# Neighbourhood attention with its projections four half-steps ahead, and modulation weights loaded two blocks at a time

## The chip, the cores and the metric

The kernel runs on one core of one Trainium2 chip. The metric is the device time of one execution in microseconds (us). An execution has five engines that work side by side, each through its own list of instructions in order: TensorE (PE; its weight loads are shown apart as PEld), VectorE (DVE), ScalarE (ACT), GpSimd (POOL) and SyncE (SP), which here only issues DMAs. Instructions wait for each other through semaphores.

## The reference, cut to what matters

The model has two layers over 512 latent tokens and 256 context tokens of width 1024. Layer 0 mixes tokens by neighbourhood attention with 16 heads of 64, layer 1 by a bidirectional recurrence (RWKV-7); each is followed by a mixture of 16 experts. Each layer is modulated: a vector of 6 x 1024 numbers per token kind is computed from a condition.

```
sh1, sc1, gt1, sh2, sc2, gt2 = split(silu(c) @ ada_w[i] + ada_b[i], 6)      # ada_w[i]: 1024 x 6144
h   = rms_norm(x, norm1_g[i]) * (1 + sc1) + sh1
q, k, v = h @ w_qkv;   q, k = rms_norm per head
s_lat = q . k(8 x 16 neighbourhood) * scale + bias(relative row, relative column);   s_ctx = q . k(context) * scale
o   = softmax([s_lat, s_ctx]) @ [v_lat, v_ctx];     x = x + gt1 * (o @ w_o)
x   = x + gt2 * experts(rms_norm(x) modulated by sh2, sc2)
```

The same is done for the context tokens, with c_ctx in place of c and attention to context alone. `ada_w` of the two layers is 50 MB in float32.

## The kernel before, in words

Layer 0's attention is `phase_na`. The 16 heads are taken as 8 pairs `p`. All matmuls of projections and scores are done in split form (a high part and a low part, three matmuls for one product, `passes`).

*Opening.* The input rows are normalised and transposed. `ada(S, 0, 0)` and `ada(S, 0, 1)` (shift and scale of layer 0) run here, with seven buffers of 512 KB for their weights, and then the modulated input is written as `hTh` and `hTl`. `na_consts` (line 217) makes the masks and loads the position biases of all 16 heads into one tile `BT` by 16 DMAs on SP.

*One modulation part.* `ada(S, l, j)` (line 117) computes one of the six parts of layer `l`. Its 1024 x 1024 weights come in 8 blocks of 128 rows, each one DMA of 512 KB on SP. For each block four matmuls (a quarter of the columns each, in a quarter of the rows of the result) go to a PSUM tile, and VectorE adds the result to `acc` (line 137); with the first block a bias is added by four more matmuls (line 133) and the result copied (line 135). After each block the generator yields. At the end two transposes and a copy give `modT`. Parts 2 to 5 of layer 0 and all six of layer 1 are left for the attention: 10 parts, 80 steps.

*One projection.* `na_project(S, p)` (line 279) loads and splits the weights (`split_weights`: ScalarE line 252, VectorE line 253), then makes queries and keys of pair `p` in six products of 24 matmuls, yielding after each. After every second product the rows are normalised (ScalarE squares into `sq`, VectorE sums, ScalarE takes the root, VectorE scales, line 305), transposed on TensorE and written as `qT`, `kT` and `kl`. For even `p` six more products give the values of two pairs.

*One pair of attention.* `na_attend(S, p)` (line 345) takes 16 half-steps. Half-steps 0 to 11 make scores (TensorE lines 357 to 367), softmax (VectorE lines 375 to 386, with the bias from `BT` at line 377; ScalarE line 384); transposes follow one step later and values (line 406) two steps later, so half-steps 12 to 15 hold only transposes and values of the last two blocks.

*The order.* `weave` (line 487) advances several generators at given rates in one loop. First projection 0 alone. Then for `p` = 0 to 6: the 16 half-steps of attention `p`, the projection of pair `p + 1` (13 steps if it has values, else 7, spread over the 16), and one modulation step per half-step, until the 80 are used up. Then the projections' memory is given back (`ew.close()`), the gate rows are made, the output weights are loaded and split (`out_weights`, 8 DMAs of 512 KB on SP), and pair 7 is attended alone. Then the rows of x are loaded again, and `out_project` and the experts follow. The order in the program is a priority: a planner puts each engine's instructions in order by it and by when their tiles are free and their inputs expected; on the chip each engine keeps that order. All the loads named here stand in one queue, SP's. A load into a tile of a pool waits until the tile's last users are done.

Of the kernel before, what the change touches and what calls it, by code (L numbers as in the profile page):

```python
# [20 lines left out]
F32 = mybir.dt.float32  # L21
# [10 lines left out]
P = 128  # L32
D = 1024
KD = 8
# [6 lines left out]
H = 16  # L41
# [9 lines left out]
def vap(ap, dims, offset=0):  # L51
    return bass.AP(tensor=ap.tensor, offset=ap.offset + offset, ap=dims)
# [64 lines left out]
def ada(S, l, j):  # L117

    nc, I = S.nc, S.I
    acc = S.small.tile([P, 256], F32, name="adam")  # L120
    adab = S.small.tile([24, 256], F32, name="adab")
    nc.gpsimd.dma_start(adab, I["ada_b"][l].rearrange("(c n) -> c n", n=256))
    for k in range(KD):
        w = S.adaw.tile([P, D], F32, name="adaw")
        nc.sync.dma_start(w, I["ada_w"][l, k * P:(k + 1) * P, j * D:(j + 1) * D])
        ps = S.ps_mm.tile([P, 512], F32, name="mm")[:, :256]
        for q in range(4):
            nc.tensor.matmul(ps[32 * q:32 * q + 32], S.sT[:, k, :], w[:, q * 256:(q + 1) * 256],
                             start=True, stop=(k > 0))
        if k == 0:  # L130
# [86 lines left out]
def na_consts(S, pool):  # L217
    nc, rp = S.nc, S.rp
    S.BT = pool.tile([P, H, 265], F32, name="BT")
    for c in range(16):  # L220
        nc.sync.dma_start(S.BT[8 * c:8 * c + 8], vap(rp, [[31, 8], [465, H], [1, 265]], c))
    S.mL = pool.tile([P, P], BF16, name="mL")
# [58 lines left out]
def na_project(S, p, hT, wp, grp, Q):  # L281
# [11 lines left out]
    Q.k = grp.tile([P, 2, 768], F32R, name="kT")  # L293
    Q.kl = S.kl[p % 2]
    w = split_weights(S, wp, "w", [(i * P, W[:, i * D + p * P:i * D + (p + 1) * P]) for i in range(2)], 3)
    for t in range(0, NT, 2):
        for ps in product(w, t):
            yield
        sq = S.small.tile([P, 2, 256], F32, name="sq", bufs=1)
        nc.scalar.activation(sq, ps, AF.Square)  # L300
# [36 lines left out]

STEPS = 16
STRIP = (0, 64, 192, 256)
# [5 lines left out]
def na_attend(S, p, Q, V, VS, OT):  # L345
# [14 lines left out]
    def scores(u):  # L360
# [5 lines left out]
        if w == 0:  # L366
# [4 lines left out]
            dots(ps[:, 256:512], s, qc, slice(512, 768), True)  # L371
            b = S.BT[:, 2 * p + s, BOFF[j]:BOFF[j] + 1]
            b = bass.AP(tensor=b.tensor, offset=b.offset, ap=[list(b.ap[0]), [-1, 32], [-31, 8]])
# [136 lines left out]
def phase_na(S):  # L510
    nc, tc, I = S.nc, S.tc, S.I
    with ExitStack() as es:
# [6 lines left out]
        S.wraw = ew.enter_context(tc.tile_pool(name="nawr", bufs=2))  # L519
        S.adaw = ew.enter_context(tc.tile_pool(name="naada", bufs=2))  # L520
        S.ps_sc = ea.enter_context(tc.tile_pool(name="ps_sc", bufs=2, space=PSUM))
# [14 lines left out]
        raw = tmp.tile([P, KD, 768], F32, name="raw")  # L536
        adaw, S.adaw = S.adaw, et.enter_context(tc.tile_pool(name="nada0", bufs=7, side="right"))
        rms_rows(S, XN, XN, raw.rearrange("p k t -> p (k t)"))
# [26 lines left out]
        def modulation():  # L565
            for l, js in ((0, range(2, 6)), (1, range(6))):
                for j in js:
                    yield from ada(S, l, j)
        mods = modulation()
        weave(1, (na_project(S, 0, (hTh, hTl), wp, grp, Q[0]), 0, 1))  # L570
        for p in range(7):
            def some():
                for _ in range(STEPS):
                    next(mods, None)
                    yield
            weave(1, (na_attend(S, p, Q[p], Q[p - p % 2].V, Q[p - p % 2].VS, OT), 0, 1),
                  (na_project(S, p + 1, (hTh, hTl), wp, grp, Q[p + 1]), 0, (13 if p % 2 else 7) / STEPS),
                  (some(), 0, 1))
        for _ in mods:
            pass  # L580
        ew.close()
# [4 lines left out]
        ws = out_weights(S, es, I["na_w_o"][0])  # L586
        weave(1, (na_attend(S, 7, Q[7], Q[6].V, Q[6].VS, OT), 0, 1))
        ea.close()
# [1357 lines left out]
```

## Time and profile before

| | us |
|---|---|
| three runs | 2753.96, 2755.37, 2766.93 (median 2755.37) |
| the profiled execution | 2758.18 |
| its span, first to last instruction | 2756.4 |
| TensorE busy, of the span | 2470.2 (90%) |
| VectorE busy | 1327.1 (48%) |
| ScalarE busy | 1004.0 (36%) |
| GpSimd busy | 591.5 (21%) |
| DMA of the hardware queues, as a share of 16 engines | 63.5% |

The profile is that of one execution. "Busy" is the time in which at least one instruction of the engine is under way; matmuls are pipelined, and one that starts 0.12 us after another is shown with a length of 0.28 us, so a busy TensorE need not be at its peak. The granted clock (PEclk) is the share of full speed that TensorE was given: 1.00 is 2.4 GHz and 0.50 is 1.2 GHz. The attention of layer 0 lies from 58 to 534 us of the span.

### The profile page before, as it was taken

The page shows a single profiled execution, that of the slowest core. Times are in us where ns is not written, and L with a number is a line of the kernel's source. Part 1 is how long each engine was busy: PE and PEld are TensorE (multiplying, and loading weights), DVE is VectorE, ACT ScalarE, POOL GpSimd, SP SyncE. Part 2 cuts the span into 40 slices and gives each one's busy share as a digit, 9 for nine tenths or more (in the row PEclk, how much of TensorE's full clock was granted, in tenths as well). Part 3 has the DMA queues.
Part 4 walks back from the last instruction along what each step waited for, and adds up shares of the span by engine and source line. Part 5 has one row for each costly group of instructions (what it writes and reads, how often), then busy time and mean ns, then how long its engine had stood idle before and what let it go on. Part 6 is the DMA issues. An engine that isn't in the chain of part 4 may idle for free. (4 is left out here: it accounts for less than half of the span.)

```text
span 2756.4 us, 44025 instructions
## 1 busy us (share of the span) xinstructions
PE 2470.2 (90%) x16800; PEld 1574.1 (57%) x16800; DVE 1327.1 (48%) x3006; ACT 1004.0 (36%) x2127; POOL 591.5 (21%) x857
## 2 busy tenths in 40 slices
PE   6998999898999999997698697999999977998887
PEld 4876879793333333333388686777777862332222
DVE  6665566642222222225978845666666771221222
ACT  3555556642111101113266634766665431000100
POOL 2100000121000000001656525665655110000000
PEclk9999999998999999998899898999999978999999
DMA  8646440328787878784157866565554369999998
GB/s 246 147 150 187 132 152 15 109 100 327 298 320 312 334 305 329 293 357 172 69 186 241 269 167 130 124 134 125 126 122 125 87 243 378 420 420 421 420 420 342
DMA packets 378371, 637.64 MB, mean 231 GB/s; under 512 B 133832, under 2 KB 301056, under 8 KB 329008
## 3 DMA queue, kind: packets, MB, share of 16 engines
q1 hardware_dynamic: 370944, 609.11, 63.5%
q0 software_dynamic: 7216, 25.70, 2.5%
q8 instruction: 134, 2.20, 0.3%
q14 instruction: 77, 0.63, 0.1%
HBM read 565.11 MB, written 53.88 MB: 225 GB/s over the span
## 5 line engine op out<-in xcount | busy, mean ns | idle before, releaser
L790 PE MATMUL P<-wm,xin 128*64 128x512 f32 x2048 | 494.3, 601 | 25.8 <-DMA wm<-in_moe_w_dram 24.7
L790 PEld LDWEIGHTS P<-wm,xin 128*64 128x64 f32 x2048 | 141.0, 137 | 328.3 <-issue 259.4
L823 PE MATMUL mm<-wm,hidT 128*64 128x512 f32 x1024 | 245.9, 601 | 16.8 <-ACT hidT L807 14.9
L801 ACT ACTIVATE hid<-P 128x512 f32<-128x512 f32 x32 | 19.1, 597 | 563.3 <-PE P L790 563.3
L763 POOL DMA_INDIRECT xg<-xnd,ii x20 | 19.7, 985 | 846.5 <-PE tp L77 571.5
L837 DVE SCALAR_TENSOR_TENSOR Y<-mm,gates,gt 64x512 f32<-64x512 f32 x64 | 48.0, 750 | 283.1 <-PE mm L823 282.4
L260 PE MATMUL mm<-wh,hTh 128*128 128x256 f32 x576 | 173.5, 302 | 1.9 <-ACT hTh L554 1.9
L802 DVE TENSOR_TENSOR hid<-P,hid 128x512 f32<-128x512 f32 x32 | 22.1, 692 | 308.3 <-PE P L790 293.6
L262 PE MATMUL mm<-wh,hTl 128*128 128x256 f32 x576 | 168.4, 293 | 1.9 <-DVE hTl L557 1.9
L261 PE MATMUL mm<-wl,hTh 128*128 128x256 f32 x576 | 168.7, 293 | 0.0
L823 PEld LDWEIGHTS mm<-wm,hidT 128*64 128x64 f32 x1024 | 72.7, 137 | 151.9 <-issue 121.3
L1477 POOL TENSOR_TENSOR Wi<-Wi,Ti 112x30 f32<-112x30 f32 (+14 forms) x240 | 141.4, 589 | 18.8
L1475 POOL TENSOR_TENSOR Ti<-Wi 112x30 f32<-112x30 f32 (+14 forms) x240 | 134.9, 562 | 18.2
L795 PE MATMUL Pc<-wm,xin 128*32 128x512 f32 x1024 | 138.5, 597 | 0.0
L260 PEld LDWEIGHTS mm<-wh,hTh 128*128 128x128 f32 x576 | 114.3, 199 | 11.9 <-issue 8.8
L262 PEld LDWEIGHTS mm<-wh,hTl 128*128 128x128 f32 x576 | 113.6, 198 | 4.5 <-DVE hTl L557 2.8
L1554 PE MATMUL mm<-FR,QF 128*128 128x128 f32 (+1 forms) x768 | 115.1, 294 | 0.4 <-ACT QF L1542 0.4
L261 PEld LDWEIGHTS mm<-wl,hTh 128*128 128x128 f32 x576 | 114.6, 199 | 1.3 <-issue 1.1
L864 DVE TENSOR_TENSOR X<-mm,X 128x512 f32<-128x512 f32 x80 | 52.6, 687 | 111.9 <-PE mm L863 111.7
L1554 PEld LDWEIGHTS mm<-FR,QF 128*128 128x128 f32 x768 | 98.7, 200 | 7.4 <-ACT QF L1542 0.9
L1542 ACT ACTIVATE QF<-mm 64x256 f32<-64x256 f32 x192 | 72.6, 378 | 67.7 <-PE mm L1538 64.3
L1557 DVE TENSOR_TENSOR FT<-mm,eye 64x128 f32<-64x128 f32 x192 | 55.8, 292 | 78.9 <-ACT FT L1556 76.6
(437 smaller groups left out, 5715.6 us busy)
## 6 DMA issues: line engine op xcount, KB each, us to landing
wm<-in_moe_w_dram SPq DMA_DIRECT2D x378, 1024.0 KB
adaw<-in_ada_w_dram SPq DMA_DIRECT2D x96, 512.0 KB
wraw<-in_na_w_qkv_dram SPq DMA_DIRECT2D x32, 256.0 KB
wm<-in_moe_w_dram POOLq DMA_DIRECT2D x6, 1024.0 KB, 10.8
pkd<-sig SPq DMA_DIRECT2D x24, 256.0 KB
pkd<-kka SPq DMA_DIRECT2D x24, 256.0 KB
pkd<-av SPq DMA_DIRECT2D x24, 256.0 KB
sig<-pkd SPq DMA_DIRECT2D x16, 384.0 KB
```

The source lines that it names most:

```text
L260: S.nc.tensor.matmul(ps, xh, wh, start=(k == 0), stop=False)
L261: S.nc.tensor.matmul(ps, xh, wl, start=False, stop=False)
L262: S.nc.tensor.matmul(ps, xl, wh, start=False, stop=(k == n - 1))
L790: nc.tensor.matmul(ps[64 * hf:64 * hf + 64], xin[:, k, cl], w[:, hf * 512:(hf + 1) * 512], start=k == 0, stop=k == KD - 1)
L795: nc.tensor.matmul(Pc[32 * i:32 * i + 32], xinc[:, k, cc], ws[k][i // 2][:, (i % 2) * 512:(i % 2 + 1) * 512], start=k == 0, stop=k == KD - 1)
L823: nc.tensor.matmul(py[64 * hf:64 * hf + 64], hT[:, k % 4, k // 4, :], ws[k][:, hf * 512:(hf + 1) * 512], start=k == 0, stop=k == KD - 1)
L864: nc.vector.tensor_tensor(X[t][:, sl], ps, X[t][:, sl], op=ALU.add)
L1475: nc.gpsimd.tensor_tensor(t, W3[:, i + 1:32, i:i + 1].to_broadcast([112, n, i]), W3[:, i:i + 1, 0:i].to_broadcast([112, n, i]), op=ALU.mult)
L1477: nc.gpsimd.tensor_tensor(W3[:, i + 1:32, 0:i], W3[:, i + 1:32, 0:i], t, op=ALU.add)
L1542: nc.scalar.activation(QF[m][0:64, u], pq[64 * u:64 * u + 64], AF.Copy)
L1554: nc.tensor.matmul(pf[:, h, s0:], QF[m][:, u, h, :], rhs, start=True, stop=True)
L1557: nc.vector.tensor_tensor(F[64:128, :, 64:128], pf[64:128, :, 64:128], S.eye2[64:128, None, :].to_broadcast([64, 2, 64]), op=ALU.add)
```

## The change

It does five things. Attention becomes one generator over all pairs, and the first weave takes only 12 of its half-steps, so that each later weave begins with the last four half-steps of the pair before, and the last stretch has 20 half-steps. `ada` loads two blocks by one DMA of 1 MB and adds up two blocks in PSUM before VectorE reads them: 4 steps per part, 40 in the attention. Four of them go into each of the seven weaves, and the last 12 beside the last stretch at a rate of 0.6 per half-step. The pool of their two tiles moves so that it lives until the last pair is done; the opening has four tiles of 1 MB for seven of 512 KB. The position biases are loaded for each pair, by two DMAs in `na_project`, into a tile with two buffers. `sq` gets a second buffer.

```diff
@@ ada
-    for k in range(KD):
-        w = S.adaw.tile([P, D], F32, name="adaw")
-        nc.sync.dma_start(w, I["ada_w"][l, k * P:(k + 1) * P, j * D:(j + 1) * D])
+    for k in range(0, KD, 2):
+        w = S.adaw.tile([P, 2, D], F32, name="adaw")
+        nc.sync.dma_start(w, I["ada_w"][l, k * P:(k + 2) * P, j * D:(j + 1) * D].rearrange("(i p) n -> p i n", p=P))
         ps = S.ps_mm.tile([P, 512], F32, name="mm")[:, :256]
-        for q in range(4):
-            nc.tensor.matmul(ps[32 * q:32 * q + 32], S.sT[:, k, :], w[:, q * 256:(q + 1) * 256],
-                             start=True, stop=(k > 0))
+        for i in range(2):
+            for q in range(4):
+                nc.tensor.matmul(ps[32 * q:32 * q + 32], S.sT[:, k + i, :], w[:, i, q * 256:(q + 1) * 256],
+                                 start=i == 0, stop=i == 1 and k > 0)
@@ na_consts
-    S.BT = pool.tile([P, H, 265], F32, name="BT")
-    for c in range(16):
-        nc.sync.dma_start(S.BT[8 * c:8 * c + 8], vap(rp, [[31, 8], [465, H], [1, 265]], c))
@@ na_project
+    Q.BT = grp.tile([P, 2, 265], F32, name="BT")
+    for s in range(2):
+        nc.sync.dma_start(Q.BT[:, s], vap(S.rp, [[1, 16], [31, 8], [1, 265]], 465 * (2 * p + s)))
...
-        sq = S.small.tile([P, 2, 256], F32, name="sq", bufs=1)
+        sq = S.small.tile([P, 2, 256], F32, name="sq")
@@ module
-STEPS = 16
+STEPS, LEAD, ADA, LASTADA = 16, 4, 4, 0.6
@@ phase_na
-        S.adaw = ew.enter_context(tc.tile_pool(name="naada", bufs=2))
+        S.adaw = ea.enter_context(tc.tile_pool(name="naada", bufs=2, side="right"))
...
-        adaw, S.adaw = S.adaw, et.enter_context(tc.tile_pool(name="nada0", bufs=7, side="right"))
+        adaw, S.adaw = S.adaw, et.enter_context(tc.tile_pool(name="nada0", bufs=4, side="right"))
...
-        mods = modulation()
+        def attention():
+            for p in range(8):
+                yield from na_attend(S, p, Q[p], Q[p - p % 2].V, Q[p - p % 2].VS, OT)
+
+        def some(gen, n):
+            for _ in range(n):
+                next(gen, None)
+                yield
+        mods, att = modulation(), attention()
         weave(1, (na_project(S, 0, (hTh, hTl), wp, grp, Q[0]), 0, 1))
         for p in range(7):
-            def some():
-                for _ in range(STEPS):
-                    next(mods, None)
-                    yield
-            weave(1, (na_attend(S, p, Q[p], Q[p - p % 2].V, Q[p - p % 2].VS, OT), 0, 1),
-                  (na_project(S, p + 1, (hTh, hTl), wp, grp, Q[p + 1]), 0, (13 if p % 2 else 7) / STEPS),
-                  (some(), 0, 1))
-        for _ in mods:
-            pass
+            n = STEPS if p else STEPS - LEAD
+            weave(1, (some(att, n), 0, 1),
+                  (na_project(S, p + 1, (hTh, hTl), wp, grp, Q[p + 1]), 0, (13 if p % 2 else 7) / n),
+                  (some(mods, ADA), 0, ADA / n))
         ew.close()
...
-        weave(1, (na_attend(S, 7, Q[7], Q[6].V, Q[6].VS, OT), 0, 1))
+        weave(1, (att, 0, 1), (mods, 0, LASTADA))
         ea.close()
```

## Rows read from the trace of the kernel before

**Rows 1.** Busy time of each engine by stretch. Columns: stretch, its length, then for PE, PEld, DVE, ACT and POOL the busy time and the number of instructions, then the granted clock, the busy share of the DMA engines and GB/s.

```profile
58.00:492.00 434.00, 416.01 (x3679) 341.58 (x3680) 261.97 (x754) 238.65 (x463) 35.12 (x78) 0.96 0.45 126
492.00:534.00 42.00, 32.75 (x252) 26.82 (x252) 32.46 (x85) 32.68 (x62) 2.49 (x5) 0.88 0.44 148
534.00:610.00 76.00, 76.00 (x670) 76.00 (x668) 27.27 (x62) 30.72 (x64) 18.94 (x27) 1.00 0.17 66
...
58.00:94.00 36.00, 35.24 (x282) 33.58 (x282) 19.28 (x37) 13.63 (x26) 6.44 (x13) 0.95 0.68 80
...
153.00:267.00 114.00, 110.57 (x1028) 87.33 (x1026) 69.59 (x208) 62.80 (x122) 8.60 (x19) 1.00 0.50 153
283.00:393.00 110.00, 108.31 (x1009) 85.83 (x1013) 67.25 (x200) 61.30 (x120) 7.56 (x17) 1.00 0.52 158
```

**Rows 2.** TensorE's instructions in order of time, from a stretch without a stall. Columns: start, length, engine, line, operation, tiles, form, number merged into the row.

```profile
300.35 0.64 PE L128 MATMUL mm<-adaw,sT 128*32 128x256 f32 x8
300.92 0.28 PE L367 MATMUL sc<-mR,mL 128*128 128x256 bf16 x1
...
305.02 0.28 PE L261 MATMUL mm<-wl,hTh 128*128 128x256 f32 x1
305.14 0.28 PE L262 MATMUL mm<-wh,hTl 128*128 128x256 f32 x1
305.35 0.64 PE L128 MATMUL mm<-adaw,sT 128*32 128x256 f32 x8
```

**Rows 3.** TensorE's instructions in order of time at the end of pair 0; in brackets the idle time before and what ended it.

```profile
137.52 0.28 PE L262 MATMUL mm<-wh,hTl 128*128 128x256 f32 x1
...
142.66 1.09 PE L77 MATMUL tp<-ident,sq 128*128 128x128 f32 x4 [1.88 <-DVE sq L305]
144.78 1.08 PE L128 MATMUL mm<-adaw,sT 128*32 128x256 f32 x8 [1.03 <-DMA adaw<-in_ada_w_dram]
...
148.71 0.58 PE L260 MATMUL mm<-wh,hTh 128*128 128x256 f32 x1
149.09 0.41 PE L261 MATMUL mm<-wl,hTh 128*128 128x256 f32 x1
149.31 0.42 PE L262 MATMUL mm<-wh,hTl 128*128 128x256 f32 x1
```

**Rows 4.** Busy time by stretch, columns as in rows 1, at the ends of pairs 0, 2 and 4.

```profile
140.00:153.00 13.00, 9.26 (x59) 6.07 (x56) 5.66 (x15) 3.98 (x7) 1.30 (x3) 0.61 0.76 241
267.00:283.00 16.00, 11.13 (x78) 7.95 (x81) 7.21 (x21) 5.37 (x10) 1.30 (x3) 0.68 0.62 199
393.00:406.00 13.00, 9.52 (x67) 7.36 (x59) 6.09 (x13) 5.24 (x8) 0.79 (x2) 0.74 0.37 121
```

**Rows 5.** TensorE's waits: engine, line, what it waited for, us in total, times, longest. The first two from 58 to 492 us, then the wait for modulation weights alone in 140 to 152, 262 to 278 and 390 to 400 us.

```profile
PE mm L128 <- DMA adaw<-in_ada_w_dram: 11.2, 9, 2.3
PE tp L77 <- DVE sq L305: 5.6, 3, 1.9
...
PE mm L128 <- DMA adaw<-in_ada_w_dram: 1.9, 2, 1.0
...
PE mm L128 <- DMA adaw<-in_ada_w_dram: 3.0, 2, 2.3
...
PE mm L128 <- DMA adaw<-in_ada_w_dram: 1.6, 1, 1.6
```

**Rows 6.** TensorE's instructions in order of time, in the last pair.

```profile
505.67 0.37 PE L367 MATMUL sc<-mR,mL 128*128 128x256 bf16 x1 [3.66 <-DVE nm L377]
...
509.42 1.12 PE L77 MATMUL tp<-ident,sb 128*128 128x128 f32 x4 [2.10 <-DVE sb L386]
```

**Rows 7.** Groups of instructions from 58 to 492 us: line, engine, operation, tiles, form, number, busy time and mean ns of one, idle time before them.

```profile
L137 DVE TENSOR_TENSOR adam<-mm,adam 128x256 f32<-128x256 f32 x70 | 29.1, 416 | 33.2 <-PE mm L128 32.9
...
L77 PE MATMUL tp<-ident,adam 128*128 128x128 f32 x20 | 4.6, 316 | 0.0
```

**Rows 8.** The loads: first SP's instructions in order of time (start, time to the end of the last merged), then the issues by tile with their number and size.

```profile
43.76 20.79 SPq L221 DMA_DIRECT2D BT<-rpbp  x16
73.99 4.23 SPq L273 DMA_DIRECT2D wraw<-in_na_w_qkv_dram  x4
...
adaw<-in_ada_w_dram SPq DMA_DIRECT2D x96, 512.0 KB
...
wraw<-in_na_w_o_dram SPq DMA_DIRECT2D x8, 512.0 KB
...
BT<-rpbp SPq DMA_DIRECT2D x16, 132.5 KB
```

**Rows 9.** TensorE's instructions in order of time, at the end of the opening's modulation.

```profile
43.07 0.64 PE L128 MATMUL mm<-adaw,sT 128*32 128x256 f32 x8 [0.63 <-DMA adaw<-in_ada_w_dram]
44.41 0.64 PE L128 MATMUL mm<-adaw,sT 128*32 128x256 f32 x8 [0.69 <-DMA adaw<-in_ada_w_dram]
45.58 0.44 PE L77 MATMUL tp<-ident,adam 128*128 128x128 f32 x2 [0.54 <-DVE adam L137]
```

**Rows 10.** Busy time by stretch, columns as in rows 1: the opening's loads, and the loads of x after the last pair.

```profile
10.00:40.00 30.00, 22.40 (x165) 10.17 (x165) 22.86 (x45) 7.66 (x11) 1.51 (x3) 1.00 1.05 381
...
532.00:538.00 6.00, 5.31 (x48) 5.07 (x46) 1.54 (x3) 2.17 (x4) 0.50 (x1) 1.00 0.88 328
```

**Rows 11.** SP's waits from 58 to 492 us, columns as in rows 5.

```profile
SPq L125 <- PE mm L128: 187.7, 68, 14.3
```

More of the change, by code (lines that the diff above doesn't have):

```diff
@@ L217, in na_consts @@
 def na_consts(S, pool):
-    nc, rp = S.nc, S.rp
-    S.BT = pool.tile([P, H, 265], F32, name="BT")
-    for c in range(16):
-        nc.sync.dma_start(S.BT[8 * c:8 * c + 8], vap(rp, [[31, 8], [465, H], [1, 265]], c))
+    nc = S.nc
     S.mL = pool.tile([P, P], BF16, name="mL")
@@ L371, in scores @@
             dots(ps[:, 256:512], s, qc, slice(512, 768), True)
-            b = S.BT[:, 2 * p + s, BOFF[j]:BOFF[j] + 1]
+            b = Q.BT[:, s, BOFF[j]:BOFF[j] + 1]
             b = bass.AP(tensor=b.tensor, offset=b.offset, ap=[list(b.ap[0]), [-1, 32], [-31, 8]])
```

## The prediction, made before the changed kernel was run

> **What bounds the kernel now.** I read the busy times of the page first: TensorE is the fullest engine. Then the busy time by stretch, to find where the changed code lies: the pairs woven with projections run from 58 to 492 us, the last pair alone from 492 to 534, the output projection from 534 to 610 [rows 1]. In the first stretch TensorE is busy 416.0 of 434 us at a mean granted clock of 0.96, and no other engine comes near (VectorE 262, ScalarE 239): this stretch is bound by TensorE's order of work. The DMA engines are at 0.45. In 492 to 534 nothing is full: TensorE 32.8, VectorE 32.5, ScalarE 32.7 of 42 us. From 534 to 610 TensorE is busy all the time. So whatever brings the output projection forward brings all that follows it forward by as much, since everything behind it waits for its tiles.
>
> Busy time of a matmul holds its latency, so I take prices from starts: a projection matmul starts 0.12 us after the one before it, a modulation block (8 instructions) gives way after 0.57 us, and the switch to it costs some 0.09 us (0.21 instead of 0.12 between the two starts) [rows 2].
>
> The lost time in the stretch has one shape. At the end of each even pair (140, 268 and 395 us) the next pair's projection has no value part, so its last q/k product is followed at once by scores that need it. TensorE waits 1.88 us for VectorE's scaled rows, then the next modulation blocks in its order wait for their DMA (1.03 us before the first; 1.9 at this place, 3.0 and 1.6 at the other two [rows 5]), and then matmuls start 0.21 us apart instead of 0.12 [rows 3]: the granted clock has gone to the lower level (1.2 GHz of 2.4) after the idle time. The three places, as length minus busy time times granted clock, lose 13 - 9.26 x 0.61 = 7.4, 16 - 11.13 x 0.68 = 8.4 and 13 - 9.52 x 0.74 = 6.0 us, together 21.8 [rows 4]. The waits of TensorE in the stretch say the same: 11.2 us for modulation weights and 5.6 us for the scaled rows are nearly all of its 18 us [rows 5]. The fourth such place is 501 to 509 us, inside the last pair: 3.66 and 2.10 us idle [rows 6]; that stretch loses 42 - 32.75 x 0.88 = 13.2 us.
>
> **The change part by part.**
>
> *Four half-steps of lead.* The last four half-steps of a pair hold no scores, only transposes and values. With the lead they stand at the head of the next weave, beside the first three half-products of the next projection (3 x 24 x 0.12 = 8.6 us) and one modulation step. From the end of the last product (137.8) to the point where TensorE ran on at 148.7 [rows 3] the old chain took 10.9 us, 1.9 of them waits for DMA; some 9 us of chain now stand over 8.6 + 1.2 us of modulation + about 2 us of tail. That covers it, barely, and the clock stays up with it. I take 85% of 21.8: 18.5 us; bounds 0 and 21.8. Next in line is the next projection's weight split, whose second half waits for a tile that the last product frees.
>
> *Modulation, two blocks at a time.* TensorE has the same instructions, 8 for a block. Before: 80 steps x (0.57 + 0.09) + 10 x 0.99 for bias and transposes (0.57 + 0.09, and 0.33 for the two transposes, 0.32 long and overlapped [rows 7]) = 62.7 us. After: 28 steps beside the projections are 56 x 0.57 + 28 x 0.09 + 7 x 0.99 = 41.4 us, so 21.3 us leave this stretch; 12 steps beside the last pair are 24 x 0.57 + 12 x 0.09 + 3 x 0.99 = 17.7 us. The 40 additions less on VectorE (0.416 us each [rows 7], 16.6 us) are worth nothing while it is busy 262 of 434 us; at most they shorten what the lead covers anyway.
>
> *Slower loads beside the projections.* 4 MB of modulation weights per pair instead of 8: the waits for them outside the three places are 11.2 - (1.9 + 3.0 + 1.6) = 4.7 us [rows 5]; I take 3 of them, bounds 0 and 5.1 (the idle time of 153 to 267 and 283 to 393 [rows 1]).
>
> *Biases per pair.* The 16 issues of 132.5 KB stay 16; before they held the SP queue from 43.8 to 64.6 us, and the weights of pair 1 went out at 74.0 [rows 8]. TensorE lost 0.8 us in 58 to 94, so nothing is gained. Two issues (0.6 us of SP) and 0.27 MB per pair now stand ahead of weights that are needed a weave later, and the pair's own biases have that weave to land in: 0, at most 2 us lost if they push the weights. The second buffer of the squares: 0 to 1 us gained, 0 taken.
>
> *Opening.* Eight loads of 1 MB in four tiles for 16 of 0.5 MB in seven. After the last landing two blocks are to do instead of one (0.64 us at 44.41, then the transposes at 45.58 [rows 9]): +0.6 us, and some more if fewer, larger tiles come free late. I take +1, bounds -1 and +3. The Trainium skill ("DMA: Bandwidth & Descriptors", section "Bandwidth") says to batch DMAs to 1 MiB for three quarters of peak, and its section on the anatomy of one DMA gives about 2 us of fixed cost each; by that, 8 loads fewer would be an estimated 16 us less here. The trace does not agree: half-megabyte loads already run at 381 GB/s with the engines full from 10 to 40 us [rows 10].
>
> *The last pair.* TensorE's useful work there is 32.75 x 0.88 = 28.8 us, and 17.7 come in: 46.5 us against 42. The tail of the pair before replaces the norm chain that it waited for, the 13.2 us of loss fall to some 3.5 (the score chains at the end stay), so 50 us: +8. VectorE gets 12 additions and copies (5 us) on 32.5, so it stays under. The DMA: 12.6 MB of modulation weights and 4.2 MB of output weights [rows 8], some 2.1 MB of it ahead of time; 14.7 MB take 39 us at the 381 GB/s of the opening and 45 at the 328 of 532 to 538 us [rows 10]. Both fit into 50. Bounds 46.5 and 65 (45 us, and 20 for output and modulation loads waiting for each other in SP's one order: an estimate from 12 loads x the 1.6 us that 0.5 MB takes at 328).
>
> **Sum** on the profiled execution (span 2756.4, with 1.8 around it 2758.2): -18.5 - 21.3 - 3 + 1 + 8 = -33.8 us, 2724. The median of the runs is 2755.4, 2.8 lower: I forecast **2721.5**.
>
> **The rivals** (on the median).
> - *Lead without cover.* The planner puts the weight splits or modulation blocks so that the three places still stall: the 18.5 stay, -15.3, **2740**. For it: ScalarE's splits wait for the product's tiles. Against: the work named above is there.
> - *The last pair is paced by its loads*: 62 us instead of 50, -21.8, **2733.5**. For it: SP has one order, and output weights wait there for VectorE's splits.
> - *All cover*: every stall goes and the last pair takes 46.5: -21.8 - 21.3 - 5.1 + 4.5 = -43.7, **2711.5**.
> - *Slower: the last pair's loads run at the pace of the woven pairs.* There 153 GB/s [rows 1], because each load waits for TensorE to give back one of two tiles (187.7 us of SP's waits [rows 11]); TensorE in turn waits for the load, with attention queued behind it and VectorE's splits behind that. 14.7 MB at 153 are 96 us, +54 instead of +8: +12, **2767**. It turns the sign once that stretch passes 84 us (175 GB/s). Against: tiles twice as large hold 2.1 MB ahead.
> - *A shorter opening*: if a load's price is per load and not per byte, eight loads fewer at the 1.34 us between the last blocks [rows 9] take 10.7 us from the opening instead of adding 1, -45.5, **2710**. The full DMA engines of [rows 10] speak against it. (This is the page's rule on batching; its 2 us each would make it 2705.)
>
> **How the numbers follow.** Forecast 0.50 (own range 2714 to 2729); no cover 0.12; last pair paced by loads 0.17; all cover 0.11; slower 0.07; shorter opening 0.03. A measurement can tell about 0.5%, here 13.8 us (below 2741.6 and above 2769.1; part of the 2767 case with worse loads passes it, and I count all of it). Faster: 0.50 + 0.11 + 0.03 and most of the two weak cases (0.05 of 0.12, 0.11 of 0.17) = 0.80; same 0.13; slower 0.07. The range reaches from 2703 to 2746: it leaves out the slower case, the far ends of the two weak ones, and little below.
>
> **What would show it.** Right: no stretch between 90 and 450 us with a granted clock near 0.6, TensorE's wait for modulation weights under 4 us up to the last projection, that projection's end near 450 us instead of 492, the first matmul of the output projection near 500 instead of 534, and the same lengths behind it. Wrong in a step: idle TensorE ahead of the scores of odd pairs (lead); over 60 us between the last projection and the output projection (loads). The whole is wrong if the output projection comes forward but the expert layer's start does not, because a tile is freed later there.

## The result, and the profile after

The changed kernel takes 2722.5 us (median of 4 runs, 2719.1 to 2727.9) against 2758.4 for the kernel before on the same chip: a ratio of 0.987, with an interval of 0.984 to 0.989. The forecast was 2721.5. The profiled execution took 2723.3 (span 2721.5), 34.9 less than that of before, where the sum of the prediction gave 33.8. The sum is right to a microsecond; its terms are not.

The windows of the changed kernel, columns as in [rows 1]: up to the last projection product, then up to the first product of the output projection; then, as places that answer to those of [rows 4], windows around the last scaled rows of pairs 1, 3 and 5, which TensorE now transposes at 137.5, 239.7 and 342.6 us.

```profile
58.00:436.30 378.30, 376.69 (x3419) 328.32 (x3417) 243.61 (x692) 225.43 (x451) 37.37 (x77) 1.00 0.38 113
436.30:499.40 63.10, 53.49 (x526) 36.73 (x524) 40.09 (x112) 35.10 (x70) 3.00 (x6) 0.89 0.74 253
...
137.00:150.00 13.00, 13.00 (x121) 11.32 (x120) 7.23 (x18) 5.59 (x13) 2.09 (x5) 1.00 0.38 122
237.00:253.00 16.00, 16.00 (x143) 13.60 (x142) 8.74 (x22) 5.69 (x13) 2.09 (x5) 1.00 0.42 137
340.00:353.00 13.00, 13.00 (x119) 10.64 (x118) 6.11 (x15) 4.04 (x10) 1.40 (x4) 1.00 0.42 131
```

The three stalls are gone: TensorE is busy all through them, at full clock. In the whole woven stretch, length less busy time times clock was 434.0 - 416.01 x 0.96 = 34.6 us before [rows 1]; it is 378.3 - 376.7 = 1.6 now. But the stretch from the last projection to the output projection has grown from 41.8 to 63.1 us. TensorE's waits say the same: the first line is the only one from 58 to 436 us, where [rows 5] had 11.2 us for weights; the second is the longest from 436 to 499.

```profile
PE mm L260 <- DVE hTl L558: 1.5, 2, 0.8
...
PE mm L129 <- DMA adaw<-in_ada_w_dram: 7.9, 5, 2.6
```

TensorE in that stretch, first a window and the longest of the waits for weights, then the end in order of time:

```profile
452.00:460.00 8.00, 5.60 (x35) 3.71 (x39) 5.14 (x21) 3.17 (x8) 0.00 (x0) 0.59 1.01 361
...
454.25 1.93 PE L129 MATMUL mm<-adaw,sT 128*32 128x256 f32 x16 [2.61 <-DMA adaw<-in_ada_w_dram]
...
482.40 1.07 PE L129 MATMUL mm<-adaw,sT 128*32 128x256 f32 x16 [0.38 <-DMA adaw<-in_ada_w_dram]
483.40 0.63 PE L134 MATMUL mm<-adab,ident 24*32 24x256 f32 x8
483.96 0.65 PE L407 MATMUL po<-PT,V 128*64 128x128 f32 x6
485.26 1.07 PE L129 MATMUL mm<-adaw,sT 128*32 128x256 f32 x16 [0.64 <-DMA adaw<-in_ada_w_dram]
488.68 1.07 PE L129 MATMUL mm<-adaw,sT 128*32 128x256 f32 x16 [2.35 <-DMA adaw<-in_ada_w_dram]
491.69 1.93 PE L129 MATMUL mm<-adaw,sT 128*32 128x256 f32 x16 [1.94 <-DMA adaw<-in_ada_w_dram]
493.56 3.78 PE L154 MATMUL mm<-ident,modT 128*128 128x128 f32 x16
...
499.36 0.36 PE L258 MATMUL mm<-o0h,oh 128*128 128x256 f32 x1
```

One wait, 2.61 us, comes early, and the clock goes to the lower level behind it (0.59 from 452 to 460 us). The last values of attention (line 407) stand at 483.96. Three modulation steps follow, each waiting for its weights. The last of them and the first gate rows (line 154) run at the lower clock: 1.93 us for sixteen matmuls that take 1.07 above.

Behind the attention the lengths are not what they were. From its first to its last product of the hidden layer (`P`) the expert layer 0 takes 610.4 us for 621.9; the recurrence with the routing (from the last scatter of the expert layer 0 to the first product of layer 1) takes 1011.8 for 1001.5. Attention -34.5, experts -11.5, recurrence +10.3: the last two cancel.

### The profile page after: what moved, and what is told of

Same layout as the page of the kernel before. It is cut to its first block, busy times and chain, and to the rows that moved or that the text cites. A ratio compares the mean times of both kernels' runs of the same rounds, so it can differ in the third digit from the quotient of the medians.

```text
span 2721.5 us, 43825 instructions
## 1 busy us (share of the span) xinstructions
PE 2454.3 (90%) x16800; PEld 1582.0 (58%) x16800; DVE 1313.6 (48%) x2958; ACT 993.0 (36%) x2121; POOL 595.7 (22%) x857
## 5 line engine op out<-in xcount | busy, mean ns | idle before, releaser
L258 PE MATMUL mm<-wh,hTh 128*128 128x256 f32 x576 | 168.0, 292 | 2.1 <-ACT hTh L555 2.1
## 6 DMA issues: line engine op xcount, KB each, us to landing
wm<-in_moe_w_dram POOLq DMA_DIRECT2D x6, 1024.0 KB, 10.7
```

Source lines behind the costliest of these rows:

```text
L258: S.nc.tensor.matmul(ps, xh, wh, start=(k == 0), stop=False)
```

## The experiments

All twelve runs beside the two kernels. The first two columns are the starts of the last projection product and of the first output projection product; then the length of the expert layer 0, all from the profiled execution; then the median of the runs.

| kernel | last projection | output projection | expert 0 | median us |
|---|---|---|---|---|
| before | 492.1 | 533.9 | 621.9 | 2756 to 2759 |
| after | 436.3 | 499.4 | 610.4 | 2722.5 |
| e4: before + lead | 466.5 | 512.5 | 623.3 | 2744.6 |
| e7: before + biases per pair | 487.2 | 529.2 | 623.6 | 2756.7 |
| e9: e7 + four single tiles | 466.9 | 510.3 | 623.4 | 2737.8 |
| e6: e7 + two blocks | 460.7 | 501.9 | 611.2 | 2709.8 |
| e11: e6 + lead | 454.2 | 500.1 | 612.1 | 2718.1 |
| e2: after - lead | 452.0 | 510.1 | 610.5 | 2724.9 |
| e1: after, 6 steps per weave | 447.6 | 487.0 | 622.5 | 2721.0 |
| e12: e1 - lead | 461.7 | 502.8 | 623.4 | 2731.5 |
| e10: e1, one `sq` | 448.5 | 491.7 | 611.0 | 2714.2 |
| e5: after, 5 steps, rate 0.25 | 447.4 | 493.4 | 622.7 | 2720.5 |
| e8: after, rate 1.0 | 436.7 | 504.6 | 622.9 | 2735.1 |
| e3: after, later loads left out | 436.9 | 490.8 | 623.5 | 2721.7 (one run) |

### What removed the stalls

**Without the lead** (e2).

```diff
-STEPS, LEAD, ADA, LASTADA = 16, 4, 4, 0.6
+STEPS, LEAD, ADA, LASTADA = 16, 0, 4, 0.75
```

> The changed kernel with LEAD = 0 (and the last 12 modulation steps at 0.75 per half-step, so that they end with the 16 half-steps that are left). Theory (the lead covers the norm chain): TensorE waits again for the scaled rows at the ends of pairs 0, 2, 4 and 6, with the low clock behind it, 4 to 6 us each: time 2738-2746. Rival (the stalls went because the modulation loads are slower and no longer wait there): no stall, time 2722 +- 4.

**The lead alone**, on the kernel before with its single blocks (e4): `attention()`, `some(att, n)` and `n` as in the change, `some(mods, n)` at a rate of one.

> The kernel before with the lead alone (one attention generator, first weave 12 half-steps); modulation in single blocks, 16 per weave, biases all at once. Theory (the lead covers the chain): the three stalls and the one at 501 us go, 22 to 30 us: time 2727-2737. Rival (the modulation loads make the stalls): TensorE waits for modulation weights at the same places, time 2750 or more.

The woven stretch of e2, then of e4, columns as in [rows 1]:

```profile
58.00:452.00 394.00, 390.68 (x3454) 332.79 (x3453) 244.36 (x702) 226.58 (x456) 35.64 (x77) 1.00 0.35 108
```

```profile
58.00:466.50 408.50, 399.51 (x3642) 330.06 (x3643) 256.97 (x744) 235.03 (x455) 36.46 (x78) 1.00 0.47 133
```

Both are at full clock: of the 34.6 us that the stretch lost before, 3.3 are left in e2 and 9.0 in e4. (e4's output projection comes 21.4 us earlier, and its profiled execution is 22.3 us shorter; the median of its ten runs, 2744.6, is only 11 us below that of before and lies between its two forecasts.) That fits a stall with two conditions: scores right behind a chain on VectorE, and a modulation block behind them in TensorE's order whose weights have not landed. The lead takes the first away (e4 keeps 6.7 us of waits for weights, in pieces of at most 1.5), the new loads take the second. So each alone removes most of the same loss: the lead brings the output projection forward by 21.4 us, two blocks by 27.3 (e7 to e6), the changed kernel with both by 34.5.

**Biases alone, two blocks, and four single tiles** (e7, e6, e9). e7 is the kernel before with the change's edits of `BT`. On it, e6 has the change's `ada` and

```diff
-                for _ in range(STEPS):
+                for _ in range(STEPS // 2):
...
-                  (some(), 0, 1))
+                  (some(), 0, 0.5))
```

so eight steps of two blocks per weave, none beside the last pair; e9 has instead

```diff
-        S.adaw = ew.enter_context(tc.tile_pool(name="naada", bufs=2))
+        S.adaw = ew.enter_context(tc.tile_pool(name="naada", bufs=4))
```

> The kernel before with the biases loaded per pair, nothing else. Theory: nothing (2750 to 2760 us; out projection within 2 us of 533.9, the three stalls as before). Rival: the 16 loads of the biases kept weights or modulation blocks late in the first pairs, and 3 us or more are gained in the woven stretch.

> The kernel before, with two blocks per load and the biases per pair (which make room for the larger tiles), without the lead and without moving steps to the last pair: 8 steps per weave, used up after five pairs, so 8 MB of modulation weights per pair as before. Theory A (the stalls at the ends of even pairs went in the run without lead because four megabytes per pair come in time where eight do not): here the stalls stay, waits of TensorE for modulation weights of 6 to 11 us up to the last projection, clock 0.6 to 0.75 at the three places, out projection at 531 to 536 us. Theory B (they went because the two larger tiles hold two megabytes ahead): waits under 2 us, clock 1.00 in the woven stretch, out projection at 510 to 518 us. The total follows: A 2755 +- 5, B 2735 to 2745.

> The kernel before with the biases per pair, and four tiles of half a megabyte for the modulation weights in place of two: single blocks, as much memory as two blocks of two. Its expert and recurrence stages have the same order of TensorE's instructions as those of the kernel before. Theory (the stalls went because two megabytes of modulation weights stand ahead in place of one): no wait of TensorE for these weights over 2 us up to the last projection, clock 0.99 or 1.00 there, out projection at 500 to 510 us; total 2725 to 2735. Rival (it is the accumulation in PSUM: half the additions on VectorE, half the changes of tile, half the switches): waits and clock as before (0.96 to 0.97), out projection at 525 to 533 us; total 2748 to 2757.

e7 changes nothing in the total (ratio 0.9998, 0.9982 to 1.0013). In its profiled execution, though, the output projection comes 4.7 us earlier, as its rival had it: the waits for weights are 4.7 us for 11.2 (and 3.5 more before the same blocks, put down to ScalarE), while those for the scaled rows are 5.6 as before. e6 and e9 show what is enough to take the waits away. The woven stretch of e7, of e6 and of e9:

```profile
58.00:487.20 429.20, 414.07 (x3680) 339.78 (x3681) 261.99 (x754) 238.54 (x463) 35.12 (x78) 0.97 0.43 129
```

```profile
58.00:460.70 402.70, 400.50 (x3698) 338.93 (x3699) 250.79 (x724) 236.23 (x465) 35.28 (x78) 1.00 0.43 135
```

```profile
58.00:466.90 408.90, 407.05 (x3693) 335.87 (x3692) 262.76 (x761) 231.57 (x461) 35.28 (x78) 1.00 0.44 133
```

e6 and e9 load as many bytes per pair as the kernel before, and both are at full clock; e9 has no wait for weights at all, and e6 one of 0.3 us. So 2 MB that stand ahead are enough, without a slower pace; whether the slower pace alone, with 1 MB ahead, would have been enough too, no run shows. Neither run waits for the scaled rows any more, though neither has the lead. Theory B of e6 held; its output projection came 8 us ahead of B's range and its total 25 us below it, some 12 of them by the order of the expert layer (below). e9 came just behind its own (510.3 us, total 2737.8). What two blocks bring beyond memory is 8.4 us at the output projection (510.3 to 501.9), 6.2 of them in the woven stretch, where all the steps stand. A step's price gives that size: in the fence of the result, sixteen matmuls start at 482.40 and the next instruction at 483.40, so two blocks take 1.00 us where single ones take 2 x 0.57, and each has one switch for two [rows 2]. That is 0.14 + 0.09 us for each of 40 steps, an estimate of 9.2 us.

### What the lead is worth then

e2 against the changed kernel says 10.7 us at the output projection (and 2.4 in the medians, 2724.9 and 2722.5). To see it with no steps beside the last pair, e11 puts the lead on e6 (and the second `sq`), and e12 takes it from e1 (and the second `sq`):

> The run with two blocks and biases per pair (no lead; 2710) with the lead of four half-steps and the second buffer of the squares put on top: eight modulation steps per weave, none beside the last pair. Its expert and recurrence stages have the same order of instructions on TensorE and VectorE as in that run. Theory (the lead fills the places where TensorE would wait at the ends, above all in the last stretch, and the 15 us by which the run with six steps reached the out projection ahead of the run without lead are its own): out projection at 486 to 490 us for 501.9, total 2693 to 2700. Rival (with the stalls gone the lead is worth nothing, and the 15 us came from spreading the modulation over seven weaves): out projection at 499 to 503, total 2706 to 2712.

> The run with six modulation steps per weave (lead, out projection at 487.0, 2721) without the lead, and with one buffer of the squares; the expert stage and the recurrence have the same order of TensorE's and VectorE's instructions as in that run. Theory A (with six steps in each of seven weaves no load is late, and the places at the ends of even pairs have a modulation step whose weights are there, so the lead is worth 2 us as it was beside eight steps per weave): out projection at 487 to 492 us, total 2720 to 2726. Theory B (the lead is worth some 11 us, as between the changed kernel and its copy without lead, and only the late load that came back hid it beside eight steps per weave): out projection at 496 to 502 us, total 2730 to 2736.

The two disagree: 1.8 us in e11, 15.8 in e12 (and 10.5 in the medians). The reason shows in e11, TensorE's windows and the wait inside them:

```profile
130.00:140.00 10.00, 6.85 (x83) 4.93 (x81) 7.32 (x16) 6.42 (x15) 0.40 (x1) 0.98 0.71 254
140.00:150.00 10.00, 8.57 (x57) 6.78 (x57) 1.40 (x3) 1.15 (x3) 0.40 (x1) 0.68 0.68 222
```

```profile
132.64 1.93 PE L129 MATMUL mm<-adaw,sT 128*32 128x256 f32 x32
...
141.43 1.94 PE L129 MATMUL mm<-adaw,sT 128*32 128x256 f32 x16 [3.17 <-DMA adaw<-in_ada_w_dram]
```

A late load came back at the end of pair 0, and with it a stall that takes 7.5 us of these 20 by length less busy time times clock. The order of the steps goes with it: e11 still gives one modulation step to two half-steps, and the lead leaves the first weave only 12 half-steps for its eight. The sixth and the seventh run in one piece at 132.64, and the eighth is the one that waits at 141.43. Even without that stall e11 would gain some 9 us, not the 15.8 of e12; its last stretch is 45.9 us long, e1's 39.4. Where no late load came back the gain is real, but it is not that of covered stalls. Theory B of e12 had the total (2731.5) and missed the output projection by 0.8 us. e12, then e1, up to the last projection and on to the output projection:

```profile
58.00:461.70 403.70, 401.84 (x3688) 337.59 (x3688) 251.90 (x719) 229.58 (x459) 37.42 (x78) 1.00 0.43 135
461.70:502.80 41.10, 31.98 (x254) 26.58 (x252) 30.74 (x85) 31.84 (x62) 2.52 (x5) 0.88 0.44 147
```

```profile
58.00:447.60 389.60, 387.61 (x3662) 333.92 (x3663) 248.51 (x714) 234.97 (x458) 39.57 (x81) 1.00 0.45 140
447.60:487.00 39.40, 34.84 (x287) 28.02 (x285) 31.95 (x92) 33.60 (x70) 0.99 (x2) 0.96 0.43 137
```

The last stretch holds four half-steps more and is still 1.7 us shorter: its loss falls from 41.1 - 31.98 x 0.88 = 13.0 to 6.0 us. The woven stretch holds 26 matmuls less and is 14.1 us shorter, with no stall in either: matmuls simply follow each other more closely (9.40 per us for 9.14). Busy time hides such spacing. What spaces them in e12 I did not find.

### The last stretch

**The loads left out** (e3), the steps and their matmuls kept:

```diff
-        w = S.adaw.tile([P, 2, D], F32, name="adaw")
-        nc.sync.dma_start(w, ...)
+        w = getattr(S, "wkeep", None)
+        if w is None:
+            w = S.adaw.tile([P, 2, D], F32, name="adaw")
+            nc.sync.dma_start(w, ...)
+            if (l, j) >= (1, 3):
+                S.wkeep = w
```

> The changed kernel without 11 of the last 12 modulation loads: the steps of layer 1's parts 3 to 5 all read the one tile that the first of them loaded, so these three parts of layer 1's modulation are computed from wrong weights; all matmuls stay. Theory (paced by loads): the last stretch falls from 63 to 46-50 us, output projection near 484, time 2705-2710. Rival (TensorE's work and the score chains): it stays at 58 or more, time 2717 or more.

```profile
436.90:490.80 53.90, 53.30 (x525) 34.26 (x523) 37.13 (x110) 35.16 (x71) 2.99 (x6) 1.00 0.26 81
```

TensorE is busy at full clock, and the stretch takes 53.9 us, between the two forecasts. So of the 63.1, the loads account for 9.2; 53.9 stay without them, and of the 21.3 us of growth the loads are the smaller half. That the 53.9 are all TensorE's own work is not shown, as a busy TensorE can hide spacing (e12).

**Six steps per weave** (e1: `ADA` 6; all 40 beside the projections), **five** (e5: `ADA` 5, `LASTADA` 0.25; five beside the last pair), **and the 12 asked for earlier** (e8: `LASTADA` 1.0):

> Six modulation steps per weave instead of four, so none of the 40 is left beside the last pair. Theory (the last stretch of the changed kernel is paced by its 12 modulation loads): the woven stretch grows by 13 steps x 1.3 = 17 us (last projection matmul at 453 instead of 436), the last stretch falls from 63 to 36-42 us, output projection at 489-495, time 2712-2718. Rival (the last stretch is long because of TensorE's added work, the loads hide): it falls only by the 17 us that moved, output projection at 499, time 2722.

> The changed kernel with five modulation steps per weave for four (35 of 40 beside the projections), and the last five beside the last pair at a rate of 0.25. Theory (the last stretch of 63.1 us is TensorE's work plus loads that come late at its end; a step costs about 1.3 us wherever it stands): the woven stretch ends near 443 us (436.3 + 7 x 1 us), no wait for modulation weights over 1 us in the last stretch, which takes 40 to 47 us; first out-projection matmul 484 to 490 us, earlier than both 499.4 (four per weave) and 487.0 (six per weave). Rival (what leaves the last stretch comes back one for one in the woven stretch): out projection at 497 to 500 us. Total: 2706 to 2715 us if the expert layer 0 takes 610 us as in the changed kernel, 2718 to 2724 if it takes 622 as with six per weave.

> The changed kernel with the 12 steps beside the last pair at one per half-step for 0.6, so that they are asked for by half-step 12 of 20. Theory (the end of the last stretch waits because modulation loads are behind the output weights in SP's one order and give back two tiles only one by one): the loads cannot come earlier, waits for them stay at 6 us or more, the last stretch takes 60 to 66 us. Rival (they stand too late in the order): waits under 3 us, last stretch 52 to 57 us, out projection at 488 to 493 us.

The steps that leave the last stretch shorten it by more than they lengthen the woven one: the 12 of e1 cost 11.3 us before the last projection (436.3 to 447.6) and give 23.7 behind it (63.1 to 39.4); the seven of e5 cost 11.1 and give 17.1, so the price is not one per step. e5 lies between, 3 us later than expected: one wait of 2.5 us for weights is left. The output projection of e1 came 2 us ahead of its range, and its total, 2721.0, is the rival's, for the reason of the next section. In e8 the waits stay (8.3 us) and the stretch grows to 67.9: asked for earlier, the loads do not come earlier. SP's rows of the changed kernel (start, time to the end of the last merged) and, from 467 to 492 us, its waits for tiles show why:

```profile
464.29 2.45 SPq L271 DMA_DIRECT2D wraw<-in_na_w_o_dram  x2
467.45 19.30 SPq L125 DMA_DIRECT2D adaw<-in_ada_w_dram  x6
...
SPq L125 <- PE mm L129: 10.0, 6, 2.7
SPq L125 <- DMA adaw<-in_ada_w_dram: 7.5, 4, 3.8
```

The last six loads of modulation weights stand behind the last output weights, and spread over 19 us: SP waits 10.0 us for TensorE to be done with a tile and 7.5 for earlier loads of these weights.

### The order of the expert layer

The attention of e1 ends 12 us ahead of that of the changed kernel, and the total is the same. The expert layer 0 is 12 us longer. Its length has two values over all these kernels, 610 to 612 and 622 to 624, and they go with the order that the planner gave TensorE there: the context products (`Pc`) stand in 56 runs of the compiled program where the layer is short and in 62 where it is long, without exception (59 and 65 in the traces). Between the scatters (line 863 before, 867 after), the kernel before, then the changed one:

```profile
719.57 1.06 PE L795 MATMUL Pc<-wm,xin 128*32 128x512 f32 x6
720.56 0.50 PE L863 MATMUL mm<-yh,pm 128*128 128x512 f32 x1
...
725.96 1.04 PE L795 MATMUL Pc<-wm,xin 128*32 128x512 f32 x2
726.93 1.94 PE L790 MATMUL P<-wm,xin 128*64 128x512 f32 x8
...
730.46 1.06 PE L795 MATMUL Pc<-wm,xin 128*32 128x512 f32 x8
731.45 0.50 PE L863 MATMUL mm<-yh,pm 128*128 128x512 f32 x1
```

```profile
689.45 2.77 PE L799 MATMUL Pc<-wm,xin 128*32 128x512 f32 x22
692.16 0.50 PE L867 MATMUL mm<-yh,pm 128*128 128x512 f32 x1
...
701.75 3.64 PE L799 MATMUL Pc<-wm,xin 128*32 128x512 f32 x32
705.32 0.75 PE L77 MATMUL tp<-ident,hid 128*128 128x128 f32 x4
```

From start to next start a run of 2 context products holds TensorE 0.97 us, of 6 0.99, of 8 0.99, of 22 2.71 and of 32 3.57. A context product takes 32 of TensorE's 128 columns. In the trace the 8 start in two groups of four, 0.45 us apart; the 2 start as far apart, one after the other. With 8 as two groups and 32 as eight, (3.57 - 0.99) / 6 gives 0.43 us for a group and 0.13 for the run itself. So a run that is cut short pays for columns that stay empty, and each run for its change. (The Trainium skill, "TensorEngine Tiling (Array Packing)", "Key Properties", says that a change of the tiling mode drains TensorE; the 0.13 us per run agree with it.)

The 11.5 us arise in the first half of the layer: from product 1 to product 513 of the 1024 of `P` it is 326.2 us before and 314.7 after, from there to the last 295.7 in both. In that first half the context products hold TensorE 70.6 us in 39 runs before and 66.3 in 33 after, those of `P` 125.6 us in 48 runs and 120.9 in 40; the rest is spread over the other products. So the context products are 4.3 of the 11.5 us, and `P`, cut short as well, 4.7.

e10 tests whether the order alone decides: e1 with one buffer of `sq` in place of two, which happens to turn the order of that layer.

```diff
-        sq = S.small.tile([P, 2, 256], F32, name="sq")
+        sq = S.small.tile([P, 2, 256], F32, name="sq", bufs=1)
```

> The run with six modulation steps per weave, with one buffer of the squares again (as before) in place of two. In the compiled program this moves the order of a later stage: the expert layer 0 of this kernel takes its context products in the 56 groups of the changed kernel, not in the 62 of the kernel before and of the run with six steps. Theory (the order of that stage, and nothing of the attention, decides 12 us of it): the attention as in the run with six steps (out projection at 485 to 489 us), expert layer 0 at 609 to 612 us for 622.5, and the total 2706 to 2712 where the recurrence takes what it took there. Rival (the length of the expert layer follows from the weights' loads in flight when it starts, so from the attention's end): 621 to 624 us, total 2719 to 2723.

The expert layer took 611.0 us for 622.5, as expected. The rival is out: the output projection of e10 starts between those of e3 (490.8) and e5 (493.4), whose expert layers take 623 us. That start came 4.7 us later than in e1, which the expectation did not have, and the total 2 us above its range. -11.5 and +4.7 make -6.8, and the medians differ by 6.8 (2714.2 and 2721.0); that the two figures are equal is chance, since in the profiled executions e10's recurrence is some 6 us longer and the times are 2720.5 and 2719.2.

### What stays open

e6 has the lowest median, 2709.8 (ratio 0.982, 0.980 to 0.985), with no lead and nothing beside the last pair. e10 (0.983, 0.981 to 0.985) cannot be told from it. Against the changed kernel (0.984 to 0.989) the intervals all but part, though e6 reaches the output projection 2.5 us later. In the profiled executions, 4.0 us apart, the difference lies in the recurrence (1004.3 us for 1011.8), whose length I could not tie to the order. e11 and e6 have the same order on all engines in that stage, yet their recurrences took 1011.9 and 1004.3 us in the profiled executions, and their medians differ by 8.3, although e11 starts the output projection 1.8 us earlier. The recurrence of e11, then of e6:

```profile
1245.50:2257.40 1011.90, 863.32 (x6152) 742.01 (x6150) 702.14 (x1517) 544.41 (x1217) 496.14 (x687) 0.89 0.57 156
```

```profile
1247.00:2251.30 1004.30, 852.02 (x6150) 730.87 (x6148) 701.73 (x1517) 542.91 (x1216) 495.19 (x686) 0.90 0.57 156
```

Busy time times clock is the same as near as two decimals tell (768 and 767 us); what differs is how long TensorE had the lower clock.

## Why the prediction was right, step by step

- **What bounds the stretch** held: what was gained up to the output projection (533.9 to 499.4) came through to the start of the expert layer (636.4 to 602.4). That all behind it comes forward by as much held in the total by luck, as -11.5 and +10.3 cancel; between the changed kernel and e1 it does not hold (12 us earlier, the same total).
- **Lead, -18.5**: the three places went, as said, but the lead was not needed for it (e2). The step failed in taking the place's first cause for its only one: the rows showed the wait for weights at the same spot, and I charged the whole loss to the chain. The lead's own worth beside the new loads is 10.7 us at the output projection: the woven stretch is 15.7 us shorter than e2's, of which some 4.6 are its own half-steps that moved behind it, and the last stretch 5.0 longer. Why the rest is denser is open (e12).
- **Modulation, -21.3**: TensorE's busy time times clock fell from 399.4 to 376.7, by 22.7. In that are also the lead's four half-steps, which left the stretch (-4.6, below), and 2.1 us more that stand behind 58 us because the opening ends later: some 20 for the modulation, the size that was forecast, as near as a clock in two decimals tells (0.005 of 416 us is 2). By the price found above, 1.00 us for two blocks and not 2 x 0.57, the term would have been an estimated 25; busy time, which hides spacing, does not decide between the two.
- **Slower loads, -3**: mis-sized, and for the wrong reason. All waits for weights went, and for that the 2 MB ahead are enough (e6, e9). With the lead's term I had 21.5 us of loss removed; it was 34.6 - 1.6 = 33.0. I had summed the three places and some of the waits, and not the whole difference of length and work that [rows 1] held.
- **Biases, 0**: right in the time (e7, where the median shows nothing). In the one trace of e7 the woven stretch is 4.9 us shorter, more than the 0 taken. They also free memory: 16 x 265 numbers per partition before, 2 x 2 x 265 now, 12.7 KB less, where the larger tiles take 8 KB more.
- **Opening, +1**: the first projection product came at 50.0 for 47.9, +2.1, inside the bounds. It is not the 1 MB loads alone: e9 keeps the opening's half-megabyte loads and starts at 50.9. The rival of a shorter opening falls with it. Batching to 1 MiB, which the Trainium skill ("DMA: Bandwidth & Descriptors", "Bandwidth") advises, gained nothing on loads that already ran at 381 GB/s [rows 10]; the figures of the Trainium skill there are for loads issued from GpSimd, and these are issued from SP.
- **Last pair, +8**: wrong; it was +21.3, and the sign that I had named for a step gone wrong, over 60 us there, came. I had 46.5 of work and 3.5 of loss. The work of the lead's own four half-steps was left out: without any modulation the stretch has 34.84 x 0.96 = 33.4 us of it in e1, where before it had 28.8, so 4.6 more. That makes 51.1; e3 took 53.9, with TensorE busy in the 2.8 between them, and the loads add 9.2. The DMA did reach 361 GB/s there (452 to 460 us), but "both fit into 50" took the loads as one stream; in SP's one order, with two tiles, they came in pieces. The rival *last pair paced by its loads* had the length right (62) and the cause in part (9.2 us). Its total, 2733.5, was wrong because the woven stretch gave back as much.
- **The same lengths behind it**: wrong by -11.5 and +10.3, of which the first goes with an order of the planner and the second is not explained.

So that the total was right to a microsecond is luck, twice over: 11.5 us too little gained from the losses of the woven stretch (21.5 for 33.0) met 13.3 too little charged to the last one (8 for 21.3), and behind the attention 11.5 us gained met 10.3 lost, which the prediction had not seen at all.

## What to carry to other kernels

Two edits that each remove the same stall do not add up (21.4 and 27.3 us alone, 34.5 together with the steps that moved): before pricing both, ask which condition of the stall each takes away, and run each alone. Size a stretch's recoverable loss from its length less busy time times clock, not from the places one has found, and remember that busy time hides matmuls that stand apart. Where a planner orders the program, a change in one stage can move another stage by as much as the change is worth (12 us here): compare lengths stage by stage, and the lists of instructions, before crediting the edit.

## What was not expected of the hardware

A run of context products (32 columns of TensorE each) has a price that short runs do not escape: 0.97 us for 2, 0.99 for 8. And in the recurrence the lower clock followed idle times of 0.46 and 0.19 us, at 1688 us of the changed kernel, first in order of time, then in 5 us windows:

```profile
1688.04 0.49 PE L1542 MATMUL mm<-RHS,TB 128*128 128x128 f32 x2 [0.46 <-ACT TB L1519]
1688.72 0.57 PE L1542 MATMUL mm<-RHS,TB 128*128 128x128 f32 x2 [0.19 <-ACT TB L1519]
...
1679.30:1684.30 5.00, 5.00 (x42) 4.17 (x41) 2.92 (x9) 3.04 (x9) 4.45 (x8) 1.00 0.13 25
1684.30:1689.30 5.00, 4.34 (x41) 3.77 (x41) 2.73 (x9) 4.53 (x14) 4.53 (x7) 0.97 0.58 125
1689.30:1694.30 5.00, 5.00 (x29) 4.30 (x29) 0.92 (x4) 2.33 (x7) 4.37 (x9) 0.50 0.66 162
1694.30:1699.30 5.00, 5.00 (x24) 4.55 (x25) 3.24 (x7) 2.75 (x7) 4.46 (x7) 0.51 0.16 14
```

The kernel before, as far behind its last scatter (445 us), was idle for longer (4.21 of 5 us busy for 4.34) and kept its clock:

```profile
1729.40:1734.40 5.00, 4.63 (x40) 3.80 (x41) 1.73 (x6) 3.07 (x11) 4.45 (x8) 1.00 0.45 97
1734.40:1739.40 5.00, 4.21 (x34) 3.28 (x33) 4.34 (x7) 4.58 (x11) 4.61 (x6) 1.00 0.76 173
1739.40:1744.40 5.00, 5.00 (x37) 4.21 (x36) 3.43 (x12) 2.82 (x8) 4.14 (x12) 1.00 1.01 187
```

Ten microseconds at 1.2 GHz in place of 2.4 cost at most five. The mean granted clock differs between executions of one kernel: 0.943 to 0.954 over eleven runs of the kernel before, whose times lie 16 us apart, twice what separates the medians of e6 and e11. What decides it no run here shows.
